# A normed input turned in 32x32 squares by VectorE and a trip through HBM instead of by TensorE

## The chip, the cores and the metric

The kernel runs on one core of one Trainium2 chip. The metric is the device time of one execution in microseconds (us), the median of several runs. Before the change it is 1411.34 us over three runs, from 1411.06 to 1411.61. All profile rows come from one profiled execution of the kernel before.

## The reference

A trunk of two layers on 512 tokens of width 1024. Cut to what matters here:

```python
def reference(x, ...):
    for i in range(2):
        xn = rmsnorm(x, norm1_g[i])             # layer 2's xn is what the change touches
        u_pool, q, k, v, g_a, g_b = split(xn @ w_in[i])
        q, k = rotary(rmsnorm(q)), rotary(rmsnorm(k))
        o = diff_attention(q, k, v, lam)        # 4 heads, chunk-causal
        merged = sigmoid(g_a) * pool_mixer(u_pool) + sigmoid(g_b) * rmsnorm(o)
        x = x + merged @ w_out[i]
        hn = rmsnorm(x, norm2_g[i])
        gate, up = split(hn @ w_ffn_in[i])
        x = x + (silu(gate) * up) @ w_ffn_out[i]
    return x
```

## The kernel before

**Tiles and products.** The 512 tokens are four tiles (0 to 3) of 128; the running sum `x` lies in SBUF as `res_88` to `res_91` (one buffer per tile). Every value that goes into a product is split into a high part and a low part (`split`: the high part is a ScalarE cast, L198; the low part a VectorE subtraction, L199), and a product of 128x1024 by 1024x512 takes 8 steps of three matmuls (`product`, L282 to L284: high by high, low weight by high, high weight by low, so that the low part of the input is first needed by the third matmul). Weights come in pieces of 128x1024 (`piece`, L212) which SP loads in the order of a plan into seven buffers; ScalarE and VectorE split them into `whi` and `wlo`.

**The handover between the layers.** The last thing layer 1 does is `ffn_out`: for each token tile it adds a finished product to `res` (L761, one add for each half of 512 columns) and then calls `normed` for that tile with the key `x1`. `normed` (L346) squares the tile with a row sum on ScalarE (L350), makes the reciprocal root by one VectorE instruction and one GpSimd power (L328, L329), scales the two halves of the tile on VectorE (L354, tile `xs`, two buffers), and defers the rest. The rest, `turn`, has TensorE transpose eight 128x128 blocks into two PSUM tiles (L303) and ScalarE and VectorE split them into `xh` and `xl`, the normed input with the width on the partitions. It is the other operand of every product in layer 2's input projection. The heads go in the order 3, 2, 1, 0 (`ORDER`), and layer 2 begins with the query and key product of head 3 for tiles 0 to 3 (`attention`, L549). Each such product ends in four squares on ScalarE (L655), a reciprocal root (L328, L329), four VectorE instructions that scale it (L659, `qn`) and a rotation.

**Who sets the order.** `later(delay, what)` puts work off until a clock that counts columns streamed by TensorE has moved on by `delay`; `need` runs it at once when something asks for its result. `normed` uses a delay of 15000 columns. The tile scheduler then sets each engine's final order by the program and its priorities, and every engine runs its own list in that order: an instruction that waits holds up all that stand behind it on its engine. SP's list holds the weight loads and all round trips through HBM.

**The other kind of transpose** is in the kernel already: `turned` (L306) has VectorE transpose 32x32 squares (L310, `near`), writes the tile to HBM (L311, `away`) and reads it back in four strips (L313), so that the squares land in their places. It is used for queries and keys, for probabilities and for head outputs, from the second head on, always with a long delay (24000 to 32000 columns) before the result is used. `squares_of` orders a destination to fit.

The attention itself scores (`scores`), turns the probabilities (`turn_prob`, splitting them into `ah` and `al`), and multiplies them by the values (`weighted`, PSUM tile `oy`), with a norm after it (L617 to L620).

Of the kernel before, what the change touches and what calls it, by code (L numbers as in the profile page):

```python
# [18 lines left out]
P = 128  # L19
# [4 lines left out]
KD = D // P  # L24
# [18 lines left out]
ORDER = (3, 2, 1, 0)  # L43
# [3 lines left out]
SCORE_WAIT, PROB_WAIT, AV_WAIT, NORM_WAIT, MERGE_WAIT = 33600, 25200, 11400, 15000, 15000  # L47
# [62 lines left out]
def trunk_kernel(  # L110
# [12 lines left out]
    nc = tc.nc  # L123
# [11 lines left out]
    def tr_ps():  # L135
        return ps.tile([P, 512], F32, name="tr", tag="tr", bufs=2)
# [59 lines left out]
    def split(hi, lo, src):  # L196

        ins = nc.scalar.copy(hi, src)  # L198
        nc.vector.tensor_sub(lo, src, hi.bitcast(F32))  # L199
        return ins  # L200
# [6 lines left out]
    def piece(raw=None):  # L207
        i = at[0]
        at[0] += 1
        if raw is None:  # L210
            raw = sb.tile([P, 2, 512], F32, name="raw", tag="raw", bufs=RAWS)
        transfers.append(nc.sync.dma_start(raw.rearrange("p a b -> p (a b)"), wts[i]))  # L212
        hi = sb.tile([P, 2, 512], F32R, name="whi", tag="whi", bufs=SPLITS)
        lo = sb.tile([P, 2, 512], F32R, name="wlo", tag="wlo", bufs=SPLITS)
        split(hi, lo, raw)
        return [(hi[:, a, :], lo[:, a, :]) for a in range(2)]
# [36 lines left out]
    def wblock(n):  # L253

        return [pair for _ in range(n // 2) for pair in piece()]
# [7 lines left out]
    def later(delay, what):  # L263
        heapq.heappush(waiting, (clock[0] + delay, count[0], what))
        count[0] += 1
# [36 lines left out]
    def transpose(dst, src):  # L302
        nc.tensor.transpose(dst, src, ident)  # L303
        clock[0] += 2 * P

    def turned(src, n, tag, bufs):  # L306

        near = sb.tile([P, n * P], F32, name="near", tag=tag, bufs=bufs)
        away = hbm.tile([P, n * P], F32, name="away", tag="away", bufs=8)
        nc.vector.transpose(near.rearrange("p (c k j) -> p k c j", c=4, k=n), src.rearrange("p (k c i) -> p k c i", k=n, c=4))  # L310
        nc.sync.dma_start(away, near)  # L311
        for c in range(4):
            nc.sync.dma_start(  # L313
                near[32 * c:32 * (c + 1), :].rearrange("i (q r) -> i q r", q=4),
                away.rearrange("(q i) (c r) -> c i q r", q=4, c=4)[c])
        return near.rearrange("p (q k j) -> p k q j", q=4, k=n)

    def squares_of(x):
        return x.rearrange("p k (q j) -> p k q j", q=4)

    def rsqrt_mean(ss, n, width, times=(1.0,), eps=None):

        r = sb.tile([P, width], F32, name="r", tag="r", bufs=4)
        part = width // len(times)
        for i, f in enumerate(times):
            cs = slice(i * part, (i + 1) * part)
            e = EPS / (f * f) if eps is None else eps[i]
            nc.vector.tensor_scalar(r[:, cs], ss[:, cs], 1.0 / (n * f * f), e, op0=ALU.mult, op1=ALU.add)  # L328
        nc.gpsimd.tensor_tensor(r, r, mhalf[:, :width], op=ALU.pow)  # L329
        return r  # L330

    def small(name, width=1):
        return sb.tile([P, width], F32, name=name, tag=name, bufs=4)

    ready = set()
# [10 lines left out]
    def normed(key, t, xh, xl, g, into=None):  # L346

        xs = sb.tile([P, D], F32, name="xs", tag="mj", bufs=2)
        ss = small("ss")
        nc.scalar.activation(xs, res[t], AF.Square, accum_out=ss)  # L350
        r = rsqrt_mean(ss, D, 1)
        for half in range(2):
            cs = slice(half * 512, (half + 1) * 512)
            nc.vector.scalar_tensor_tensor(xs[:, cs], res[t][:, cs], r, g[half], op0=ALU.mult, op1=ALU.mult)  # L354

        def turn():
            tvs = []
            for half in range(2):
                tp = oy.rearrange("p a b -> p (a b)") if t == NT - 1 and not half else tr_ps()
                for i in range(4):  # L360
                    k = half * 4 + i
                    transpose(tp[:, i * P:(i + 1) * P], xs[:, k * P:(k + 1) * P])
                tv = tp.rearrange("p (k c) -> p k c", k=4)
                tvs.append(tv)
                if into is None:
                    ks = slice(half * 4, half * 4 + 4)
                    copied = split(xh[:, ks, t * P:(t + 1) * P], xl[:, ks, t * P:(t + 1) * P], tv)
            if into is not None:
                copied = into(t, tvs)
            ready.add((key, t))  # L370
            return copied

        later(NORM_WAIT, turn)

    class Quarters:

# [46 lines left out]
    def new_xT():  # L423
        xh = sb.tile([P, KD, S], F32R, name="xh", tag="xh")
        xl = sb.tile([P, KD, S], F32R, name="xl", tag="xl")
        return xh, xl
# [30 lines left out]
    xh, xl = new_xT()  # L457
# [77 lines left out]
    for layer in range(L):  # L535
# [13 lines left out]
        def attention(j, before, then):  # L549
# [88 lines left out]
            at_start = not layer and j == ORDER[0]  # L638
            near_end = at_start or j == ORDER[-1]
            if not at_start:  # L640
                w = wblock(KD)
            for t in range(NT):
                if at_start:
                    acc = first_acc[t]
# [11 lines left out]
                r = rsqrt_mean(ss, QK, 4, (QK ** -0.5, 1.0), None if layer else [stats[:, i, t:t + 1] for i in (3, 4)])  # L656
# [14 lines left out]
            w = wblock(KD)  # L671
# [234 lines left out]
        def project_out(heads, last):  # L906
            w = [wblock(2 * len(heads)) for cb in range(2)]
            if last:
                quarters.append(Quarters())
                g = gain_row(2 * layer + 1)  # L910
                early.extend(Ffn(f0) for f0 in (0, 2))
                for f in early:
                    f.gate_raw(0)
                for f in early:
                    f.gate_raw(1)
                for f in early:
                    f.gate(0, f.n11)
                with tc.issue_after(last_merged[0].ins), tc.issue_after(last_merged[1].ins):
                    early[0].gate_in("u")
            for t in range(NT):  # L920
                for cb in range(2):
                    added = add_out([((ms[j][0][:, a, token(t)], ms[j][1][:, a, token(t)]), w[cb][2 * i + a])
                                     for i, j in enumerate(heads) for a in range(2)], t, cb)
                if last and t == 1:
                    with tc.issue_after(last_merged[0].ins), tc.issue_after(added.ins):
                        early[1].gate_in("ah", "al", "pwh", "pwl")
                if last:
                    normed(f"h{layer}", t, None, None, g, quarters[-1].put)
# [12 lines left out]
        for i, j in enumerate(ORDER):  # L941
            then = (lambda: project_out(ORDER[i - 2:i - 1], False)) if i >= 2 else None
            mjs[j] = attention(j, ORDER[i - 1] if i else None, then)
            if i:
                mix(i - 1)
# [22 lines left out]
        def ffn_out(f0, f1, last):  # L968
            nonlocal xh, xl
            for cb in range(2):  # L970
                w = wblock(f1 - f0)
                if last and cb and layer + 1 < L:
                    xh, xl = new_xT()
                    g = gain_row(2 * layer + 2)
                for t in range(NT):
                    end = last and layer == L - 1
                    add_out([((hidden[f][0][:, token(t)], hidden[f][1][:, token(t)]), w[f - f0]) for f in range(f0, f1)],
                            t, cb, 2 if end and cb and t == NT - 1 else 1, end)
                    if last and cb and not end:
                        normed(f"x{layer + 1}", t, xh, xl, g)  # L980
# [67 lines left out]
```

## Time and profile before

| | |
|---|---|
| median of three runs | 1411.34 us (1411.06 to 1411.61) |
| the profiled execution | 1411.17 us, its span 1409.4 us |
| TensorE (PE) busy | 1403.4 us |
| VectorE (DVE) busy | 1023.0 us |
| ScalarE (ACT) busy | 686.8 us |
| GpSimd (POOL) busy | 118.2 us |
| granted TensorE clock | 1.0 |

The busy times are those of the whole span. A row of the timeline reads: start in us, length in us, engine, source line, operation, output and inputs, count, and in brackets the engine's idle time just before it and what ended it. Consecutive instructions of an engine overlap in these rows (a matmul of 512 columns is listed with 0.39 us and the next one starts 0.23 us after it), so the spacing of starts is what an engine can keep up, and the length is when a result is there. "SPq" and "ACTq" are the engines as issuers of DMAs. The handover lies at about 690 to 740 us.

### The profile page before, as it was taken

To read this page: it belongs to the slowest core of one execution; us is meant where nothing else is said; L and a number is where in the kernel's file an instruction comes from. 1 tells how busy PE (TensorE), PEld (TensorE's weight loads), DVE (VectorE), ACT (ScalarE), POOL (GpSimd) and SP (SyncE) were. 2 spreads that over 40 slices of the span, in tenths; PEclk is the share of its full clock that TensorE was granted. 3 is DMA by queue.
4 is the path that set the end of the run, shared out by engine and by line. 5 is a ranking of instruction groups with operands and counts; after the bars stand their busy time and mean duration, and the time that the engine had idled before them with its cause. 6 is when DMAs were issued, how large, how long until landed. Compare 5 with 4: busy or idle time off the path is not lost.

```text
span 1409.4 us, 21870 instructions
## 1 busy us (share of the span) xinstructions
PE 1403.4 (100%) x8156; PEld 1239.0 (88%) x8156; DVE 1023.0 (73%) x1915; ACT 686.8 (49%) x1309; POOL 118.2 (8%) x144
## 2 busy tenths in 40 slices
PE   9999999999999999999999999999999999999999
PEld 7888888888999899989888888888889998999897
DVE  7779787687998548737578787767769975676462
ACT  6554343443766346526354543435447662563350
POOL 1010000100001001000010101000010000010000
PEclk9999999999999999999999999999999999999999
DMA  9345353443278357629335355434424682685351
GB/s 363 104 130 148 121 164 108 141 147 84 75 180 208 111 132 183 190 49 235 120 115 170 117 168 166 142 112 154 145 45 120 161 231 73 150 185 160 99 141 60
DMA packets 104219, 201.11 MB, mean 143 GB/s; under 512 B 32688, under 2 KB 56752, under 8 KB 104112
## 3 DMA queue, kind: packets, MB, share of 16 engines
q1 hardware_dynamic: 94176, 166.14, 36.6%
q0 software_dynamic: 8640, 31.46, 12.6%
q10 hardware_dynamic: 1296, 2.11, 0.5%
q8 instruction: 64, 1.05, 0.3%
q14 instruction: 43, 0.35, 0.1%
HBM read 183.02 MB, written 16.65 MB: 142 GB/s over the span
## 4 chain that ended last, share of the span: by engine, by line
PE 95%; DVE 2%; DMA 1%; issue 0%; POOL 0%; ACT 0%; SPq 0%; DVEq 0%; POOLq 0%; ACTq 0%
PE mm L282 19%; PE mm L284 19%; PE mm L283 19%; PE mm L296 6%; PE mm L297 6%; PE mm L294 6%; PE sc L294 3%; PE sc L297 3%; PE sc L296 3%; PE tr L297 1%; PE tr L296 1%; PE tr L294 1%; PE tr L303 1%; PE sc L284 1%; PE sc L283 1%; PE sc L282 1%
## 5 line engine op out<-in xcount | busy, mean ns | idle before, releaser
L198 ACT CAST whi<-raw 128x1024 fp32r<-128x1024 f32 (+1 forms) x225 | 234.6, 1047 | 212.6 <-issue 92.9
L199 DVE TENSOR_TENSOR wlo<-raw,whi 128x1024 fp32r<-128x1024 f32 (+1 forms) x225 | 271.8, 1215 | 74.2 <-ACT whi L198 71.5
L282 PE MATMUL mm<-whi,xh 128*128 128x512 f32 x480 | 188.7, 393 | 0.0
L283 PE MATMUL mm<-wlo,xh 128*128 128x512 f32 x480 | 187.2, 390 | 0.0
L284 PE MATMUL mm<-whi,xl 128*128 128x512 f32 x480 | 187.2, 390 | 0.0
L761 DVE TENSOR_TENSOR res<-mm,res 128x512 f32<-128x512 f32 (+1 forms) x97 | 65.7, 682 | 113.2 <-PE mm L284 113.2
L284 PE MATMUL mm<-whi,fl 128*128 128x512 f32 (+1 forms) x358 | 138.5, 387 | 0.0
L282 PE MATMUL mm<-whi,fh 128*128 128x512 f32 (+1 forms) x358 | 138.3, 387 | 0.0
L283 PE MATMUL mm<-wlo,fh 128*128 128x512 f32 (+1 forms) x358 | 138.2, 387 | 0.0
L329 POOL TENSOR_TENSOR r<-r,mhalf 128x1 f32<-128x1 f32 (+1 forms) x76 | 63.8, 840 | 614.5 <-DVE r L328 493.5
L284 PEld LDWEIGHTS mm<-whi,xl 128*128 128x128 f32 x480 | 90.1, 188 | 19.2
L283 PEld LDWEIGHTS mm<-wlo,xh 128*128 128x128 f32 x480 | 90.3, 188 | 17.4
L282 PEld LDWEIGHTS mm<-whi,xh 128*128 128x128 f32 x480 | 90.2, 188 | 17.4
L238 POOL DMA_DIRECT2D wlo<-in_wts x60 | 52.6, 876 | 604.3 <-ACT wlo L237 290.4
L282 PE MATMUL mm<-xh,whi 128*128 128x512 f32 x256 | 100.4, 392 | 0.0
L283 PE MATMUL mm<-xl,whi 128*128 128x512 f32 x256 | 99.8, 390 | 0.0
L284 PE MATMUL mm<-xh,wlo 128*128 128x512 f32 x256 | 99.8, 390 | 0.0
L296 PE MATMUL mm<-xql,whi 128*128 128x256 f32 x352 | 99.7, 283 | 0.0
L294 PE MATMUL mm<-xqh,whi 128*128 128x256 f32 x352 | 99.6, 283 | 0.0
L297 PE MATMUL mm<-xqh,wlo 128*128 128x256 f32 x352 | 99.6, 283 | 0.0
L294 PE MATMUL sc<-xqh,whi 128*128 128x256 f32 x320 | 90.7, 283 | 0.0
L294 PE MATMUL mm<-xrh,whi 128*128 128x256 f32 x320 | 90.6, 283 | 0.0
(243 smaller groups left out, 3512.1 us busy)
## 6 DMA issues: line engine op xcount, KB each, us to landing
raw<-in_wts SPq DMA_DIRECT2D x244, 512.0 KB, 4.3
wlo<-in_wts POOLq DMA_DIRECT2D x60, 512.0 KB, 7.6
away<-near SPq DMA_DIRECT2D x35, 256.0 KB, 2.4
near<-away SPq DMA_DIRECT2D x140, 64.0 KB, 2.1
away<-near SPq DMA_DIRECT2D x27, 128.0 KB, 1.8
near<-away SPq DMA_DIRECT2D x108, 32.0 KB, 2.3
xr<-in_x_t SPq DMA_DIRECT2D x4, 512.0 KB, 7.0
res<-in_x SPq DMA_DIRECT2D x4, 512.0 KB, 9.0
```

The lines of the kernel that those rows point to most:

```text
L198: ins = nc.scalar.copy(hi, src)
L199: nc.vector.tensor_sub(lo, src, hi.bitcast(F32))
L238: nc.gpsimd.dma_start(lo.rearrange("p a b -> p (a b)"), wts[piece_no], accum_op=ALU.add)
L282: nc.tensor.matmul(acc, lhsT=ah, rhs=bh, start=i == 0, stop=False)
L283: nc.tensor.matmul(acc, lhsT=ah, rhs=bl, start=False, stop=False)
L284: nc.tensor.matmul(acc, lhsT=al, rhs=bh, start=False, stop=i == n - 1)
L294: nc.tensor.matmul(acc[:, i, :], lhsT=ah, rhs=bh, start=start and not i and not k, stop=False, skip_group_check=True)
L296: nc.tensor.matmul(acc[:, i, :], lhsT=ah, rhs=bl, start=False, stop=False, skip_group_check=True)
L297: last = nc.tensor.matmul(acc[:, i, :], lhsT=al, rhs=bh, start=False, stop=i == 1 and k == 3, skip_group_check=True)
L303: nc.tensor.transpose(dst, src, ident)
L329: nc.gpsimd.tensor_tensor(r, r, mhalf[:, :width], op=ALU.pow)
L761: added = nc.vector.tensor_add(res[t][:, cs], here, res[t][:, cs])
```

## The change

`normed` for layer 2's input (the case `into is None`; the three other norms, which pass a function `into`, stay as they are) no longer uses TensorE. Right after each half of `xs` it calls `turned`: a VectorE transpose of 32x32 squares into a `near` tile, a write to HBM issued by ScalarE, and four reads issued by SP. The deferred part, `placed`, only splits from `near` into `xh` and `xl`. The `near` tiles have the tags pr0 and pr1 with two buffers each, so that tile 2 takes those of tile 0. In the second layer the loading of the query and key weights of the second head in order (head 2) is placed behind the last of these reads on SP. TensorE has 32 transposes fewer, and with them the clock that sets deferred work counts 8192 columns fewer.

```diff
-    def turned(src, n, tag, bufs):
+    returned, last_x = [], []
+
+    def turned(src, n, tag, bufs, queue=nc.sync):
...
         nc.vector.transpose(near.rearrange("p (c k j) -> p k c j", c=4, k=n), src.rearrange("p (k c i) -> p k c i", k=n, c=4))
-        nc.sync.dma_start(away, near)
+        queue.dma_start(away, near)
         for c in range(4):
-            nc.sync.dma_start(
+            returned[:] = [nc.sync.dma_start(
                 near[32 * c:32 * (c + 1), :].rearrange("i (q r) -> i q r", q=4),
-                away.rearrange("(q i) (c r) -> c i q r", q=4, c=4)[c])
+                away.rearrange("(q i) (c r) -> c i q r", q=4, c=4)[c])]
...
         r = rsqrt_mean(ss, D, 1)
+        nears = []
         for half in range(2):
             cs = slice(half * 512, (half + 1) * 512)
             nc.vector.scalar_tensor_tensor(xs[:, cs], res[t][:, cs], r, g[half], op0=ALU.mult, op1=ALU.mult)
+            if into is None:
+                nears.append(turned(xs[:, cs], 4, f"pr{half}", 2, nc.scalar))
+                last_x[:] = returned
+
+        def placed():
+            for half in range(2):
+                ks = slice(half * 4, half * 4 + 4)
+                split(*(squares_of(x[:, ks, t * P:(t + 1) * P]) for x in (xh, xl)), nears[half])
+            ready.add((key, t))
...
-                tv = tp.rearrange("p (k c) -> p k c", k=4)
-                tvs.append(tv)
-                if into is None:
-                    ks = slice(half * 4, half * 4 + 4)
-                    copied = split(xh[:, ks, t * P:(t + 1) * P], xl[:, ks, t * P:(t + 1) * P], tv)
-            if into is not None:
-                copied = into(t, tvs)
+                tvs.append(tp.rearrange("p (k c) -> p k c", k=4))
+            into(t, tvs)
             ready.add((key, t))
-            return copied
-
-        later(NORM_WAIT, turn)
+
+        later(NORM_WAIT, placed if into is None else turn)
...
             if not at_start:
-                w = wblock(KD)
+                with ExitStack() as behind:
+                    if layer and j == ORDER[1]:
+                        behind.enter_context(tc.issue_after(last_x[0].ins))
+                    w = wblock(KD)
```

How this moves instructions shows at three places. The new lines are numbered differently: L350 becomes L352, L354 becomes L357, L761 becomes L770, L328 becomes L330, L310 becomes L312, L311 becomes L313, L313 becomes L315, L655 becomes L664, L659 becomes L668.

The first place is ScalarE at the handover. Before, its list runs so (`res_88` to `res_91` are tiles 0 to 3, `tr` is the PSUM tile with the transposes):

```order
L350 ACTIVATE xs,ss<-res_88 128x1024
L350 ACTIVATE xs,ss<-res_89 128x1024
L198 CAST xh<-tr 128x4x128 x2
L350 ACTIVATE xs,ss<-res_90 128x1024
L198 CAST whi<-raw 128x1024
L198 CAST xh<-tr 128x4x128 x2
L198 CAST whi<-raw 128x1024 x2
L350 ACTIVATE xs,ss<-res_91 128x1024
```

Now it runs so (the DMA rows are the writes to HBM):

```order
L352 ACTIVATE xs,ss<-res_88 128x1024
L313 DMA away<-near 128x512 x2
L352 ACTIVATE xs,ss<-res_89 128x1024
L313 DMA away<-near 128x512 x2
L352 ACTIVATE xs,ss<-res_90 128x1024
L198 CAST xh<-near 128x4x128
L198 CAST whi<-raw 128x1024 x3
L198 CAST xh<-near 128x4x128
L313 DMA away<-near 128x512
L352 ACTIVATE xs,ss<-res_91 128x1024
L198 CAST xh<-near 128x4x128
L313 DMA away<-near 128x512
```

Each pair of writes stands in ScalarE's list between the squares of two tiles, and tile 0's first cast stands behind the squares of tile 2, where before it stood ahead of them.

The second place is VectorE at the handover. Before, from the add of tile 1 on:

```order
L761 TENSOR_TENSOR res_89<-mm,res_89 128x512
L328 TENSOR_SCALAR r<-ss 128x1
L354 SCALAR_TENSOR_TENSOR xs<-res_89,r,g 128x512 x2
L199 TENSOR_TENSOR xl<-tr,xh 128x4x128 x2
L761 TENSOR_TENSOR res_90<-mm,res_90 128x512
L706 MEMSET up 128x16 x2
L714 MEMSET us 128x16 x2
L328 TENSOR_SCALAR r<-ss 128x1
L354 SCALAR_TENSOR_TENSOR xs<-res_90,r,g 128x512 x2
L199 TENSOR_TENSOR xl<-tr,xh 128x4x128 x2
```

Now, from the transposes of tile 0 on, to tile 0's first `xl`:

```order
L312 STREAM_TRANSPOSE near<-xs 128x4x4x32 x2
L770 TENSOR_TENSOR res_89<-mm,res_89 128x512
L330 TENSOR_SCALAR r<-ss 128x1
L357 SCALAR_TENSOR_TENSOR xs<-res_89,r,g 128x512 x2
L312 STREAM_TRANSPOSE near<-xs 128x4x4x32 x2
L770 TENSOR_TENSOR res_90<-mm,res_90 128x512
L715 MEMSET up 128x16
L723 MEMSET us 128x16 x2
L715 MEMSET up 128x16
L330 TENSOR_SCALAR r<-ss 128x1
L357 SCALAR_TENSOR_TENSOR xs<-res_90,r,g 128x512
L199 TENSOR_TENSOR xl<-near,xh 128x4x128
```

And a little further on, from the scaling of tile 3 to the first `xl` of tile 2:

```order
L357 SCALAR_TENSOR_TENSOR xs<-res_91,r,g 128x512 x2
L199 TENSOR_TENSOR xl<-near,xh 128x4x128
L312 STREAM_TRANSPOSE near<-xs 128x4x4x32 x2
L330 TENSOR_SCALAR r<-ss_7446 128x2 x2
L668 SCALAR_TENSOR_TENSOR qn<-mm,r,hg 128x128 x4
L442 TENSOR_TENSOR m_7459<-qn,tab 128x128
L199 TENSOR_TENSOR xl<-near,xh 128x4x128
```

The add of the next tile stands behind the two transposes of the tile before; tile 0's low part stands behind the first scaling of tile 2; and tile 2's low part stands behind the four scalings of the first finished query and key product.

The third place is VectorE in the second layer's attention, where tile 2's probabilities of head 3 are split (`al`) and head 2's queries and keys are scaled (`qn`). Before:

```order
L328 TENSOR_SCALAR r<-sso 128x1
L310 STREAM_TRANSPOSE near<-qn 128x4x4x32
L619 SCALAR_TENSOR_TENSOR mt<-oy,r,hg 128x256
L199 TENSOR_TENSOR al<-near,ah 128x384
L620 SCALAR_TENSOR_TENSOR mt<-tb,mt 128x256
L310 STREAM_TRANSPOSE near<-mt 128x2x4x32
L328 TENSOR_SCALAR r<-ss_8042 128x2 x2
L659 SCALAR_TENSOR_TENSOR qn<-mm,r,hg 128x128 x4
```

Now:

```order
L625 SCALAR_TENSOR_TENSOR mt<-oy,r,hg 128x256
L312 STREAM_TRANSPOSE near<-qn 128x4x4x32
L626 SCALAR_TENSOR_TENSOR mt<-tb,mt 128x256
L312 STREAM_TRANSPOSE near<-mt 128x2x4x32
L330 TENSOR_SCALAR r<-ss_8067 128x2 x2
L668 SCALAR_TENSOR_TENSOR qn<-mm,r,hg 128x128 x4
L199 TENSOR_TENSOR al<-near,ah 128x384
L442 TENSOR_TENSOR m_8080<-qn,tab 128x128
```

The low part of the probabilities now stands behind the four scalings of a product that ends only when TensorE has finished it. On SP, the 32 reads of the four tiles stand together ahead of five of the six weight loads that were queued there before, and those stand ahead of the round trips of the first queries and keys.

## The prediction

> **What bounds the kernel now.** I read the page first: busy times, the granted clock, the chain that ended last. Then the table of windows, and then the timelines of TensorE, VectorE, ScalarE, GpSimd and SP around the handover. From the page, busy time by engine, the clock in 40 slices, and the chain by engine:
>
> ```profile
> PE 1403.4 (100%) x8156; PEld 1239.0 (88%) x8156; DVE 1023.0 (73%) x1915; ACT 686.8 (49%) x1309; POOL 118.2 (8%) x144
> PEclk9999999999999999999999999999999999999999
> PE 95%; DVE 2%; DMA 1%; issue 0%; POOL 0%; ACT 0%; SPq 0%; DVEq 0%; POOLq 0%; ACTq 0%
> ```
>
> TensorE is busy all the time at the full clock, and the chain is TensorE. From the windows, the handover and the first attention of layer 2 (length, then busy time of PE, PEld, DVE, ACT, POOL, clock, DMA share, GB/s):
>
> ```profile
> 690.00:740.00 50.00, 50.00 (x240) 41.60 (x238) 35.82 (x79) 23.67 (x60) 7.06 (x8) 1.00 0.35 113
> 740.00:840.00 100.00, 99.71 (x478) 83.34 (x478) 81.35 (x220) 50.06 (x137) 9.71 (x12) 1.00 0.48 149
> ```
>
> TensorE does not pause at the handover: 50.00 of 50 us. So each TensorE instruction taken away there is a gain at its full price, and each result that comes later than TensorE asks for it is a loss at its full price.
>
> **What the change removes.** The transposes in the chain (start, share of the chain in us):
>
> ```profile
> 702.18 0.87 PE tr L303 x8
> ...
> 716.52 0.44 PE oy L303 x4
> 716.95 0.44 PE tr L303 x4
> ```
>
> Tiles 0 to 2 have eight transposes for 0.87 us each, tile 3 twice four for 0.44. That is 4 x 0.88 = 3.5 us, all on the path: **-3.5 us**, if nothing else comes late.
>
> **What it adds on the way to tile 0.** Before, `xs` needs 4 us to reach TensorE's first product with it. The rows of VectorE and GpSimd, of TensorE, and of ScalarE:
>
> ```profile
> 697.25 0.15 DVE L328 TENSOR_SCALAR r<-ss 128x1 f32<-128x1 f32 x1 [1.22 <-ACT xs L350]
> 698.14 1.41 DVE L354 SCALAR_TENSOR_TENSOR xs<-res,r,g 128x512 f32<-128x512 f32 x2 [0.74 <-POOL r L329]
> 699.48 0.68 DVE L761 TENSOR_TENSOR res<-mm,res 128x512 f32<-128x512 f32 x1
> 703.58 1.28 DVE L199 TENSOR_TENSOR xl<-tr,xh 128x512 fp32r<-128x512 f32 x2
> 721.43 0.71 DVE L310 STREAM_TRANSPOSE near<-qn 128x512 f32<-128x512 f32 x1
> ```
> ```profile
> 697.55 0.56 POOL L329 TENSOR_TENSOR r<-r,mhalf 128x1 f32<-128x1 f32 x1 [36.43 <-DVE r L328]
> 717.35 1.01 POOL L329 TENSOR_TENSOR r<-r,mhalf 128x4 f32<-128x4 f32 x1 [2.38 <-DVE r L328]
> ```
> ```profile
> 702.81 0.47 PE L282 MATMUL mm<-whi,fh 128*128 128x512 f32 x1
> 703.13 0.39 PE L283 MATMUL mm<-wlo,fh 128*128 128x512 f32 x1
> 703.36 0.40 PE L284 MATMUL mm<-whi,fl 128*128 128x512 f32 x1
> 709.33 0.39 PE L282 MATMUL mm<-whi,xh 128*128 128x512 f32 x1
> ```
> ```profile
> 696.07 1.06 ACT L350 ACTIVATE xs<-res 128x1024 f32<-128x1024 f32 x1 [3.75 <-DVE res L761]
> 697.03 0.18 ACT L350 ACTIVATION_READ_ACCUMULATOR xs<-res 128x1 f32 x1
> 702.66 1.08 ACT L198 CAST xh<-tr 128x512 fp32r<-128x512 f32 x2 [1.31 <-PE tr L303]
> 708.50 2.08 ACT L198 CAST whi<-raw 128x1024 fp32r<-128x1024 f32 x2
> ```
>
> and the round trip, which this kernel makes for queries, from SP's timeline (issue of the write, issue of the reads) and from the DMA list (KB each, median us from issue to landing), with ScalarE's only kind of DMA issue so far:
>
> ```profile
> 722.17 0.33 SPq L311 DMA_DIRECT2D away<-near  x1
> 724.20 1.75 SPq L313 DMA_DIRECT2D near<-away  x4
> ```
> ```profile
> near<-away SPq DMA_DIRECT2D x140, 64.0 KB, 2.1
> ```
> ```profile
> 763.45 0.33 ACTq L696 DMA_DIRECT2D pwr<-in_pool_w  x1
> ```
>
> A write is 724.20 - 722.17 = 2.03 us until its first read goes out, four reads take 1.75 us of SP, and the last lands 2.1 us after its issue at +1.3: a round trip is 2.0 + 1.3 + 2.1 = 5.4 us. VectorE's transpose is 0.71 us long, 0.62 apart in a pair (its neighbours in the rows start 0.1 us before it ends).
>
> Tile 0: `xs` is done at 699.55, the transposes at 700.2 and 700.8, the first half's round trip at 705.7. TensorE, without the 16 transposes of tiles 0 and 1, reaches the first product with `xh` at 709.33 - 2 x 0.88 = 707.6. So the trip alone would be in time, by 1.9 us less a cast. What makes it late are the queues. ScalarE first has to issue the two writes, then to square tile 1, which waits for an add that now stands behind two transposes (700.8 instead of 699.48): add until 701.45, squares and sum 1.14 until 702.65, reciprocal root 0.15 + 0.15 + 0.56, `xs` of tile 1 from 703.6 to 705.0, its transposes until 706.2, its writes on ScalarE at 705.65 and 706.3. Only then tile 2: add until 706.8, squares until 708.0. The first cast stands behind that: 708.0 to 708.6. TensorE waits 708.65 - 707.6, some **1.1 us**. The low part stands on VectorE behind tile 2's reciprocal root and first scaling (708.2, 708.9, 709.65): 709.65 to 710.3. TensorE asks for it two matmuls of 0.23 us after the first, at 709.1: **1.2 us** more. The second half is cast behind three weight casts (0.95 us each by 2.08 for two) at 711.4 to 712.0, its low part behind a scaling, a transpose, an add and a weight split at 714.1, and TensorE asks at 713.1: **1.0 us**.
>
> **Tiles 1 to 3.** Tile 1's data has been back since 711.5 or so, and its casts come as soon as ScalarE is free: 0.1. Tile 2 shares tile 0's `near` buffers, so it could be transposed only after tile 0's `xl`; and its own `xl` stands on VectorE behind the four scalings of tile 0's query and key product, which wait for that product and what follows it:
>
> ```profile
> 715.87 0.28 ACT L655 ACTIVATE qn<-mm 128x128 f32<-128x128 f32 x1 [1.70 <-PE mm L284]
> 718.40 1.13 DVE L659 SCALAR_TENSOR_TENSOR qn<-mm,r,hg 128x128 f32<-128x128 f32 x4 [1.19 <-POOL r L329]
> ```
>
> The product ends at 707.6 + 3.3 of waits + 24 x 0.2275 = 716.4; four squares 1.1 us; the reciprocal root behind tile 3's transposes at 720.9; the power 1.2; the scalings 1.1; `xl` 0.65: 724.4. TensorE is done with tile 1 at 722.4: **2.0 us**. Tile 3's writes leave ScalarE at about 720 and its `xl` again follow scalings: 0.2 + 0.1 + 1.0 = **1.4 us** by the same steps. Handover in all: 1.1 + 1.2 + 1.0 + 0.1 + 2.0 + 1.4 = **+6.8 us**. Bounds: 0 if the casts are in time after all, 8.2 by the same steps if each landing takes 4 us (see the rivals).
>
> The five weight loads that now stand behind the 32 reads leave SP near 725 instead of before 715. They serve head 2's queries and keys, which TensorE reaches only after head 3's four query and key products and four value products, 8 x 5.5 us after 707.6, about 751: 4.3 us of landing and 2.3 of splitting are covered by 20 us.
>
> **Later in layer 2.** The clock that sets deferred work counts 8192 columns fewer, so that pieces are placed elsewhere. The one place that the trace prices is the low part `al` of head 3's tiles 2 and 3. Before:
>
> ```profile
> 771.22 0.55 DVE L199 TENSOR_TENSOR al<-near,ah 128x384 fp32r<-128x384 f32 x1
> 773.90 1.13 DVE L659 SCALAR_TENSOR_TENSOR qn<-mm,r,hg 128x128 f32<-128x128 f32 x4 [1.20 <-POOL r L329]
> ```
> ```profile
> 778.61 0.28 PE L283 MATMUL oy<-vl,ah 128*128 128x256 f32 x1
> 779.06 0.39 PE L284 MATMUL oy<-vh,al 128*128 128x256 f32 x1 [0.17 <-DVE al L199]
> ```
>
> `al` comes ahead of the scalings, and TensorE loses 0.3 us at tile 3 (0.45 us from start to start, where such matmuls follow each other in 0.12). After, tile 2's `al` stands behind the scalings of a product that ends just before TensorE wants it: squares 1.1, a backlog of about 0.7 on VectorE, power 1.2, scalings 1.1, `al` 0.6, with some 0.1 us at each of five steps from engine to engine 5.2 us after that product, while TensorE has 15 matmuls of 0.23 to do, 3.5: it waits **1.7**. Tile 3 follows likewise, behind a weight split: **0.9**, against the 0.3 of before that goes. The rest of the attention is ordered differently up to about 850 us; single waits like these there I bound by 0 and 3 us and take **1.5**, the middle, since either may be.
>
> **The sum** against the profiled execution's own 1411.17 us (span 1409.4): -3.5 + 6.8 + 1.7 + 0.9 - 0.3 + 1.5 = +7.1, so 1418.3; the median of the runs shown lies 0.2 higher, and I say **1418.4 us**.
>
> [...]
>
> **The rivals.**
>
> *Full gain (the other side).* If tile 0's chain were 2.8 us shorter, so that its first `xl` were done by 707.6, and the later `xl` came ahead of the scalings, the waits would stay at a few tenths: 1411.3 - 3.5 = 1407.8. For it speaks that the bare round trip is back at 705.7, and that ScalarE is idle for much of the stretch; it decides at tile 0's first cast, which the order puts behind tile 2's squares. Against it: that order, and the adds behind transposes.
>
> *Handover only.* The later waits vanish in slack (VectorE is idle 19 us of the 100 from 740 to 840): -3.5 + 6.8 - 0.3 = +3.0, 1414.4.
>
> *The trips are slower.* Landing is not always at its median. The lists of the write's and the reads' lines over 720 to 760 us and the whole run give, in this order:
>
> ```profile
> DMA to landing us min/median/max: 1.7/2.2/5.3
> ...
> DMA to landing us min/median/max: 1.6/2.2/6.0
> ```
>
> With 4 us for each, tile 0 is back at 709.5 and the waits add up by the same steps to 12.6, in place of 6.8 + 1.7 + 0.9 + 1.5 = 10.9: 1420.1. Eight lots of 256 KB on an otherwise half idle DMA speak against it. [...]
>
> [...]
>
> **How the numbers follow.** A measurement here tells about 0.2% (2.8 us) from no change: same is 1408.5 to 1414.2. Forecast 0.57 (own range 1416 to 1421.5), handover only 0.17, full gain 0.12, slower trips 0.09, clock 0.05. The range 1412.0 to 1422.5 takes in forecast, handover only and slower trips, and leaves out the full gain and the clock (0.17). Faster is the full gain, 0.12; same is the lower half of handover only and a little of the full gain's edge, 0.10; slower the rest, 0.78.
>
> **What would show it.** Right: no L303 row near 700; PE waits at the first `xh` and `xl`, ended by ACT and DVE, together near 7 us between 705 and 735; tile 1's squares near 701.5, tile 2's near 707; `al` waits of 1 to 2 us near 780. Wrong: PE without a pause there, or waits ended by a DMA, or a PEclk below 1.

## The result, and the profile after

The changed kernel takes 1418.86 us (median of six runs, 1418.40 to 1419.29) against 1411.32 us before: 1.0052 times, 95% interval 1.0043 to 1.0062, so 7.5 us slower. The profiled execution took 1419.0 us, its span is 1417.2.

The page's busy times, and the windows that answer to those shown of before, with the one behind them:

```profile
PE 1405.0 (99%) x8124; PEld 1236.2 (87%) x8124; DVE 1027.2 (72%) x1923; ACT 686.8 (48%) x1309; POOL 117.6 (8%) x144
```
```profile
690.00:740.00 50.00, 46.09 (x192) 36.28 (x191) 37.38 (x79) 20.75 (x49) 6.06 (x7) 0.97 0.42 137
740.00:840.00 100.00, 97.85 (x461) 80.82 (x460) 77.85 (x217) 49.68 (x142) 9.25 (x12) 1.00 0.48 150
840.00:1040.00 200.00, 199.14 (x924) 165.12 (x923) 144.24 (x341) 86.62 (x216) 13.37 (x17) 1.00 0.47 147
```

TensorE now pauses for 3.9 us at the handover, where it had none, for 2.2 in the next 100 us (0.3 before) and 0.9 in the 200 after (none before). The clock column says 0.97 for the handover: for a part of it TensorE did not run at full clock. Whom TensorE waited for, from 690 to 860 us (total, times, longest):

```profile
PE mm L284 <- DVE xl L199: 3.1, 3, 1.4
PE oy L284 <- DVE al L199: 1.9, 2, 1.3
PE mm L282 <- ACT xh L198: 0.8, 1, 0.8
PE mm L283 <- DVE wlo L199: 0.6, 1, 0.6
PE oy L284 <- DVE us L723: 0.3, 1, 0.3
PE sc L283 <- DVE ql L199: 0.2, 1, 0.2
```

What ends TensorE's waits is VectorE and ScalarE each time, never a DMA. TensorE's timeline at the handover (the number behind the start is the length of the row):

```profile
707.52 0.39 PE L284 MATMUL mm<-whi,fl 128*128 128x512 f32 x1
708.70 0.50 PE L282 MATMUL mm<-whi,xh 128*128 128x512 f32 x1 [0.79 <-ACT xh L198]
709.04 0.40 PE L283 MATMUL mm<-wlo,xh 128*128 128x512 f32 x1
710.46 0.79 PE L284 MATMUL mm<-whi,xl 128*128 128x512 f32 x1 [1.02 <-DVE xl L199]
711.05 0.63 PE L282 MATMUL mm<-whi,xh 128*128 128x512 f32 x1
711.48 0.63 PE L283 MATMUL mm<-wlo,xh 128*128 128x512 f32 x1
...
722.80 0.40 PE L283 MATMUL mm<-wlo,xh 128*128 128x512 f32 x1
724.61 0.50 PE L284 MATMUL mm<-whi,xl 128*128 128x512 f32 x1 [1.41 <-DVE xl L199]
...
734.41 0.40 PE L282 MATMUL mm<-whi,xh 128*128 128x512 f32 x1
735.50 0.50 PE L284 MATMUL mm<-whi,xl 128*128 128x512 f32 x1 [0.69 <-DVE xl L199]
```

The idle time in brackets is less than what a wait costs, because the rows' lengths overlap; from start to start the four waits take 1.18, 1.42, 1.81 and 1.09 us where 0.23 is usual, 4.6 us too much. From 710.46 on, one step from matmul to matmul takes 0.59 and the six up to 713.61 take 0.43 us each, instead of 0.23. A window over that stretch shows the granted clock at half:

```profile
710.40:713.60 3.20, 3.14 (x7) 2.48 (x8) 3.20 (x6) 2.86 (x6) 0.00 (x0) 0.50 0.59 187
```

On ScalarE (first fence; ACTq are its DMA issues, and the time before such a row in which it waits for VectorE is not shown as idle) and VectorE (second) the order of the lists can be read off:

```profile
700.46 0.93 ACTq L313 DMA_DIRECT2D away<-near  x2
701.63 1.06 ACT L352 ACTIVATE xs<-res 128x1024 f32<-128x1024 f32 x1 [4.17 <-DVE res L770]
705.76 0.92 ACTq L313 DMA_DIRECT2D away<-near  x2
706.99 1.06 ACT L352 ACTIVATE xs<-res 128x1024 f32<-128x1024 f32 x1 [4.21 <-DVE up L715]
708.05 0.60 ACT L198 CAST xh<-near 128x512 fp32r<-128x512 f32 x1
...
720.62 0.92 ACTq L313 DMA_DIRECT2D away<-near  x2
721.71 0.62 ACT L198 CAST xh<-near 128x512 fp32r<-128x512 f32 x1 [2.73 <-DMA near<-away]
```
```profile
699.72 1.30 DVE L312 STREAM_TRANSPOSE near<-xs 128x512 f32<-128x512 f32 x2
700.95 0.65 DVE L770 TENSOR_TENSOR res<-mm,res 128x512 f32<-128x512 f32 x1
...
709.05 0.75 DVE L357 SCALAR_TENSOR_TENSOR xs<-res,r,g 128x512 f32<-128x512 f32 x1 [0.72 <-POOL r L331]
709.72 0.69 DVE L199 TENSOR_TENSOR xl<-near,xh 128x512 fp32r<-128x512 f32 x1
...
722.50 1.12 DVE L668 SCALAR_TENSOR_TENSOR qn<-mm,r,hg 128x128 f32<-128x128 f32 x4 [1.19 <-POOL r L331]
...
723.86 0.69 DVE L199 TENSOR_TENSOR xl<-near,xh 128x512 fp32r<-128x512 f32 x1
```

The row at 721.71, tile 2's first cast, names a DMA as what ended ScalarE's idle time. But the four reads that this cast needs went out from 714.35 to 715.64 and landed within 2.2 us, before ScalarE was free at 719.0. What held the cast are the two writes ahead of it in the list (720.62), which waited for VectorE's transposes of tile 3.

Tile 0's trip was in time. SP's first four reads and the landing of the reads (issue to landing, minimum, median, maximum) between 699 and 727 us:

```profile
702.62 1.75 SPq L315 DMA_DIRECT2D near<-away  x4
```
```profile
DMA to landing us min/median/max: 1.8/1.9/2.7
```

The last of the four went out at 702.62 + 1.3 and landed, by the median, 1.9 later, at about 705.8: 5.4 us after the write, and 2.2 us before the cast at 708.05, which stood behind the squares of tile 2.

### The profile page after: what moved, and what is told of

It is laid out like the page before. It is cut to its first block, busy times and chain, and to the rows that moved or that the text cites. A ratio compares the mean times of both kernels' runs of the same rounds, so it can differ in the third digit from the quotient of the medians.

```text
span 1417.2 us, 21898 instructions
## 1 busy us (share of the span) xinstructions
PE 1405.0 (99%) x8124; PEld 1236.2 (87%) x8124; DVE 1027.2 (72%) x1923; ACT 686.8 (48%) x1309; POOL 117.6 (8%) x144
## 5 line engine op out<-in xcount | busy, mean ns | idle before, releaser
L770 DVE TENSOR_TENSOR res<-mm,res 128x512 f32<-128x512 f32 (+1 forms) x97 | 65.7, 681 | 113.3 <-PE mm L284 113.2
```

Source lines behind the costliest of these rows:

```text
L770: added = nc.vector.tensor_add(res[t][:, cs], here, res[t][:, cs])
```

## The experiments

Times are medians, the ratio is to the kernel before on the same chip, with its 95% interval; the changed kernel's 1418.86 us is the other mark.

**1. No turning at all.**

```diff
-                nears.append(turned(xs[:, cs], 4, f"pr{half}", 2, nc.scalar))
-                last_x[:] = returned
+                nears.append(xs[:, cs].rearrange("p (k c) -> p k c", k=4))
...
+                clock[0] += 8 * P     # in placed(), for each half
```

> Leaves out the turning of layer 2's input altogether (the high and low parts are split straight from the scaled tile, so the output is not the reference's), and lets the clock count the 8192 columns as before, so that TensorE's order is that of before without the 32 transposes. If the transposes lay on the path at 0.88 us a tile: 1411.3 - 3.5 = 1407.8 us, no wait of TensorE at the handover above 0.3 us, clock 1.00. If they were hidden or the gain is eaten by something other than lateness: 1411 us.

Measured: 1408.08 us, 0.9978 (0.9969 to 0.9987), 3.1 us faster. The handover's window:

```profile
690.00:740.00 50.00, 50.00 (x225) 41.35 (x224) 37.53 (x86) 24.38 (x61) 7.38 (x8) 1.00 0.39 127
```

This kernel also leaves out VectorE's transposes, the trip and the load order behind the reads. TensorE does not pause at the handover, and the transposes are gone from its path: the gain is real. Two waits of 0.4 and 0.5 us in the attention, against 0.2 before, cover the missing 0.4 us.

**2. Tile 0 first in the queues.**

```diff
+        with ExitStack() as behind:
+            if into is None and t == 2:
+                for ins in placed_at[0, 0]:        # tile 0's first cast and low part
+                    behind.enter_context(tc.issue_after(ins.ins))
+            nc.scalar.activation(xs, res[t], AF.Square, accum_out=ss)
+            r = rsqrt_mean(ss, D, 1)
```

> The changed kernel, with tile 2's squares queued behind tile 0's first cast on ScalarE, and tile 2's reciprocal root and first scaling behind tile 0's first low part on VectorE. Theory of the queues: tile 0's trip is back near 706, so the cast comes before 707.4 and the two waits there (0.95 and 1.19 us by start to start) and the half clock behind them (1.6 us) go, at most 1 us comes back at later tiles: 1415 to 1416 us against 1418.9. Theory that the trip itself is too long: the waits stay, ended by a DMA, 1418.9 us.

Measured: 1418.28 us, 1.0048 (1.0035 to 1.0060), near the second expectation, but by neither theory. ScalarE's list and TensorE's two waits:

```profile
706.41 1.05 ACT L198 CAST whi<-raw 128x1024 fp32r<-128x1024 f32 x1 [3.99 <-PE mm L284]
707.36 0.61 ACT L370 CAST xh<-near 128x512 fp32r<-128x512 f32 x1
707.88 1.05 ACT L356 ACTIVATE xs<-res 128x1024 f32<-128x1024 f32 x1
```
```profile
708.03 0.50 PE L282 MATMUL mm<-whi,xh 128*128 128x512 f32 x1 [0.48 <-ACT xh L370]
709.38 0.50 PE L284 MATMUL mm<-whi,xl 128*128 128x512 f32 x1 [0.61 <-DVE r L330]
```

The cast did come ahead of tile 2, at 707.36, but the scheduler put a weight cast into the gap, and that weight's low part ahead of tile 0's on VectorE. Both waits shrink, from 0.79 and 1.02 to 0.48 and 0.61 us, still without a DMA as releaser; so the trip is not the limit there. There is no half clock in the profiled execution (1.00 from 690 to 740 us). The waits for later low parts of layer 2's input are 2.4 us in four places, where the changed kernel has 2.1 in two, and the `al` waits stay (1.8 us); so little of the gain shows in the time.

**3. `al` ahead of head 2's scalings.**

```diff
+                    if layer and j == ORDER[1] and not h and last_al:
+                        behind.enter_context(tc.issue_after(last_al[0].ins))
                     nc.vector.scalar_tensor_tensor(
                         qn[:, h, :], acc[:, h * QK:(h + 1) * QK], r[:, h:h + 1], g, op0=ALU.mult, op1=ALU.mult)
```

> The changed kernel, with head 2's scalings queued behind the low parts al of head 3 on VectorE. Theory of the queues: the waits for al near 777.5 and 786.8 (1.44 and 0.85 us beyond the usual 0.12) shrink to the 0.3 of before: 1418.9 - 2.0 = 1416.9 us, the handover unchanged. Rival, that the probabilities' own round trip comes back too late there (it stands behind other DMAs on SP): the waits stay, ended by ScalarE's cast or a DMA, 1418.9 us.

Measured: 1415.89 us, 1.0032 (1.0020 to 1.0043): 3.0 us less than the changed kernel, where 2.0 was expected. From 740 to 900 us TensorE waits only

```profile
PE mm L283 <- DVE wlo L199: 0.8, 1, 0.8
PE oy L284 <- DVE us L728: 0.2, 1, 0.2
```

The waits for `al` are gone. The order in VectorE's list, not a late round trip, made them. All waits in this stretch together fall from 3.0 to 1.0 us, the 2.0 expected; the further 1.0 us between the medians was not traced.

**4. The clock counts as before.**

```diff
                 split(*(squares_of(x[:, ks, t * P:(t + 1) * P]) for x in (xh, xl)), nears[half])
+                clock[0] += 8 * P
```

> The changed kernel, with the clock that sets deferred work counting the 8192 columns of the transposes that are gone. The prediction's reason for the later waits is that the clock counts fewer columns: then the later waits (about 4.5 us from 777 to 854) go and the time is about 1414.5 us. Rival: the order on VectorE there comes from how the scheduler weighs the round trips, not from the clock; the low part al still stands behind the scalings in this kernel's list, so the time is 1417 to 1419 us.

Measured: 1419.63 us, 1.0060 (1.0047 to 1.0072). The longest entry from 740 to 900 us:

```profile
PE oy L284 <- DVE al L199: 2.3, 2, 1.8
```

The waits stay. The count of columns is not what put `al` behind the scalings. In the first experiment, which counts them too but has no trip, `al` stands ahead of them without any edit, and so it does in the fifth, which does not count them. Both leave out two things together, the trips and the load order behind the reads (the plain form of experiment 10, with one trip and no load order, also keeps the order of before). So the scheduler answers to one of these two or to both; which, and by which of its rules, was not tried.

**5. VectorE's transposes without the trip.**

```diff
+        trip = queue is nc.sync
+        if trip:
             queue.dma_start(away, near)
-        for c in range(4):
+        for c in range(4 if trip else 0):
```

> Leaves out the trip through HBM (no write, no reads; the 32x32 squares stay where VectorE turned them, so the output is not the reference's) and with it the load order behind the reads. VectorE keeps all eight transposes. Theory that the trip and what it holds up in the queues make the loss: the waits at the handover fall below 1 us in sum, 1408 to 1410 us. Rival, that VectorE's extra 5 us of transposes make it the bound at the handover: the waits for the low parts stay above 3 us in sum, 1412 to 1415 us.

Measured: 1411.40 us, 1.0001 (0.9992 to 1.0010). The handover's window:

```profile
690.00:740.00 50.00, 49.53 (x220) 40.39 (x219) 39.50 (x86) 23.61 (x60) 7.38 (x8) 1.00 0.34 110
```

VectorE has more to do there than in the changed kernel (39.5 against 37.4 us), and TensorE pauses for 0.5 us instead of 3.9. So eight transposes do not make VectorE the bound at the handover; the pause there comes with the trip, the load order and the lists that the scheduler makes for them. These three go together in this experiment and are not told apart by it. The time lies between the two expectations, because waits elsewhere appeared: 2.2 us between 740 and 840 us, ended by a probability, a head output and an `al`. So even without the trip the change gains nothing: 3.3 us of the first experiment's gain are lost with VectorE's transposes in the program (and the columns not counted), and the trip with its load order costs another 7.5.

**6. Writes on SP,** with `al` ahead as in 3.

```diff
-                nears.append(turned(xs[:, cs], 4, f"pr{half}", 2, nc.scalar))
+                nears.append(turned(xs[:, cs], 4, f"pr{half}", 2))
```

> The changed kernel with the low parts al ahead of the scalings as in the third experiment (1415.9 us), and the eight writes issued by SP instead of ScalarE. If ScalarE's queue, held by writes that wait for VectorE, makes a good part of the handover's waits (the cast of tile 2's first half, 2.7 us late): 1413 to 1414.5 us. Rival, that SP is held in the same way, with the reads behind it: 1415.5 to 1417 us.

Measured: 1424.59 us, 1.0093 (1.0079 to 1.0106), 8.7 us worse than the third experiment, worse than either expectation. SP's list:

```profile
702.21 3.64 SPq L315 DMA_DIRECT2D near<-away  x8
705.94 6.39 SPq L313 DMA_DIRECT2D away<-near  x3
712.42 3.73 SPq L315 DMA_DIRECT2D near<-away  x8
```

The third of the three writes in the middle row is tile 2's; it waits for VectorE, and tile 1's reads behind it go out at 712.42, where the changed kernel has them from 708.1. TensorE waits 9.6 us for `xh` and `xl`. After two of these waits, 0.74 us at 710.81 and 1.62 at 721.69, its clock falls to half (0.50 from 711 to 714 us, and from 722.28 to 727.40 the matmuls again follow each other in 0.43); by the spacing of the matmuls that costs some 4.4 us more, so that the 8.7 us are not the price of the held reads alone.

**7. All order edits together,** with tile 3's writes on SP.

```diff
-                nears.append(turned(xs[:, cs], 4, f"pr{half}", 2, nc.scalar))
+                nears.append(turned(xs[:, cs], 4, f"pr{half}", 2, nc.sync if t == 3 else nc.scalar))
...
+                        if layer and j == ORDER[0] and not t and not h:
+                            behind.enter_context(tc.issue_after(placed_at[2, 0][1].ins))
```

> The changed kernel with all order edits together: tile 0's first cast and low part ahead of tile 2, tile 3's writes on SP, tile 2's low part ahead of head 3's first scalings, al ahead of head 2's scalings. If queue order alone makes the loss, the handover's waits fall from about 6 to 2 us or less: 1411 to 1412.5 us. Rival, that the trip of 5.4 us plus transposes, casts and low parts leaves no slack whatever the order, so that waits come back at other tiles: 1414.5 to 1416 us.

Measured: 1423.95 us, 1.0089 (1.0076 to 1.0103). TensorE's longest wait, and ScalarE's list in front of its releaser:

```profile
730.10 0.50 PE L282 MATMUL mm<-whi,xh 128*128 128x512 f32 x1 [2.47 <-ACT xh L370]
```
```profile
728.40 0.28 ACT L672 ACTIVATE qn<-mm 128x128 f32<-128x128 f32 x1 [5.03 <-DVE near L312]
...
729.42 0.63 ACT L370 CAST xh<-near 128x512 fp32r<-128x512 f32 x1
```

Now tile 3's first cast stands behind squares that wait 5 us for VectorE to free a buffer, and TensorE's clock fell to half behind its wait (0.51 from 731 to 737 us). The time is above both expectations. The forced orders do not make this: experiment 11 has the same orders, differs only in that tile 3's writes stay on ScalarE, and takes 1414.87 us. There ScalarE's list is

```profile
723.99 0.62 ACT L370 CAST xh<-near 128x512 fp32r<-128x512 f32 x1 [0.81 <-DMA near<-away]
730.03 0.28 ACT L672 ACTIVATE qn<-mm 128x128 f32<-128x128 f32 x1 [5.42 <-DVE near L312]
```

with the cast ahead of squares that wait just as long. So the move of tile 3's two writes to SP costs 9.1 us, and what it changed in view is the place of that cast.

**8 and 10. Tile 1 alone in the new way,** in two forms: with the edit to `al` of experiment 3, and plainly.

```diff
-            if into is None:
+            if into is None and t in (1,):
                 nears.append(turned(xs[:, cs], 4, f"pr{half}", 2, nc.scalar))
...
-        later(NORM_WAIT, placed if into is None else turn)
+        later(NORM_WAIT, placed if into is None and t in (1,) else turn)
```

> The kernel before, with tile 1 alone turned in the new way (eight transposes fewer on TensorE), the clock counting its columns, and al ahead of head 2's scalings. Both theories of lateness leave tile 1 in time, since its data is back 3 us or more before TensorE wants it: 1411.2 - 0.9 = 1410.3 us, at most 0.4 us of new waits. If any trip at this place disturbs the rest: over 1411.5 us.

> Tile 1 alone in the new way as in the eighth experiment (1412.3 us), without its edit to al and without the load order behind the reads, so that VectorE and TensorE keep the order of before in the attention. If the eighth lost its 0.9 us to the edits in the attention: 1410.3 to 1410.6 us, faster than before by 0.6 to 0.9. If the trip of one tile costs it elsewhere: 1411.2 us or more.

Measured: 1412.26 us, 1.0007 (0.9999 to 1.0016), and 1412.23 us, 1.0008 (0.9999 to 1.0017). The handover is undisturbed in both; this is the plain one:

```profile
690.00:740.00 50.00, 49.90 (x235) 41.23 (x234) 37.50 (x82) 23.88 (x60) 6.55 (x8) 1.00 0.44 144
```

The tile is in time, and still the 0.9 us do not show; both second expectations hold by their times. In the plain kernel's trace TensorE waits 0.8 us for `al` after the handover, 0.2 before; that takes 0.6 of it back and leaves about 1410.9. The profiled execution took 1411.65, the lowest of eleven, so 0.8 us in it stay open, and 1.3 to the median; the interval includes no change. No version that was run and computes the whole beats the kernel before.

**9. Tile 2's low part first,** on top of experiment 3: the last two added lines of experiment 7 alone.

> The third experiment's kernel (al ahead of head 2's scalings, 1415.9 us), and tile 2's first low part ahead of the four scalings of head 3's first product on VectorE; tile 3's writes stay on ScalarE. If the place of this low part is what makes tile 2's wait of 1.6 us: the wait near 723 falls to 0.3 us or less, 1414.5 to 1415 us. Rival, that its cast, which stands behind ScalarE's waiting writes of tile 3, is the real limit: the wait stays above 1.2 us, 1415.5 to 1416 us.

Measured: 1414.54 us, 1.0023 (1.0014 to 1.0032), 1.35 us less than the third experiment. TensorE's waits in the handover are down to the two at tile 0:

```profile
708.49 0.50 PE L282 MATMUL mm<-whi,xh 128*128 128x512 f32 x1 [0.79 <-ACT xh L366]
710.24 0.50 PE L284 MATMUL mm<-whi,xl 128*128 128x512 f32 x1 [1.02 <-DVE xl L367]
```

The place behind the scalings was tile 2's wait.

**11. Tile 0 first, too,** experiments 2 and 9 together.

> The ninth experiment's kernel, with tile 0's first cast and low part ahead of tile 2's squares and scaling as in the second experiment. If order edits add up: the waits at tile 0 and tile 2 are both small, 1413 to 1414 us. If each moves its wait to a later tile, as in the second and seventh experiments: 1414.5 to 1416.5 us, with waits for low parts in tiles 1 to 3.

Measured: 1414.87 us, 1.0028 (1.0017 to 1.0039), no better than the ninth. VectorE's low parts are late six times:

```profile
PE mm L284 <- DVE xl L371: 3.4, 6, 1.0
```

The edits do not add up, as the second expectation has it. Bringing tile 0 forward delays tile 2's scaling (710.06, in the changed kernel 709.05), and with it, it seems, what follows.

## Why the prediction was right, point by point

- **The gain, -3.5 us.** Shown by experiment 1: 3.1 us, with waits of 0.9 us in the attention against 0.2 before.
- **Tile 0, 1.1 + 1.2 + 1.0 us.** From start to start the first two waits cost 0.95 and 1.19 us, ended by the cast behind tile 2's squares and the low part behind tile 2's scaling, as forecast; the times of the rows agree within 0.2 us (cast 708.0 forecast, 708.05 in the trace; trip 5.4 us in both). The third did not appear in this execution: the half clock slowed TensorE by 1.6 us over the stretch in which it would have waited. Experiment 4, with the same lists at the handover and full clock (1.00 from 690 to 740 us), shows that wait with 0.58 us in its row, 0.74 from start to start.
- **Tiles 1 to 3, 0.1 + 2.0 + 1.4 us.** Measured: none, 1.6 (1.7 with the slow step behind it), 0.9. Experiment 9 shows that the scalings held up tile 2's low part. Two sums of the working do not come out: the terms for tile 2 behind 720.9 (1.2, 1.1 and 0.65) lead to 723.85 and not 724.4, so to some 1.4 us in place of 2.0, and tile 3's 0.2 + 0.1 + 1.0 is 1.3. That ScalarE's waiting writes also held tile 2's cast (721.71) was not in the working; experiment 9's cast comes hardly earlier (721.50), and the wait is gone, so it did not decide.
- **Head 3's `al`, 1.7 + 0.9 us.** Measured 1.44 and 0.85 beyond the usual 0.12, at 779.1 and 787.8. The mechanism is shown by experiment 3.
- **The rest of the attention, 1.5 us.** Measured 2.6 from start to start (a late `wlo` near 852 with 0.74 and slow steps behind it, the rest in waits of 0.2 to 0.5), less 0.4 that the kernel before loses in the same stretch: 2.2. The forecast took the middle of a bound of 0 to 3 us and named no place, so that it came near is luck.
- **The reason given for the later waits** was wrong: "The clock that sets deferred work counts 8192 columns fewer, so that pieces are placed elsewhere." With the count restored, experiment 4 keeps them. The two `al` places came out because they were read from the lists themselves.
- **The rivals.** *Full gain* decided at tile 0's first cast, and that came late. *Handover only* failed by the 4 us after the handover. *Slower trips*: landing was 1.9 us at the median at the handover and 2.2 over the run, and no wait of TensorE was ended by a DMA. The clock had 0.05 among the chances, which was the author's estimate: the trace of before has 1.00 at the handover and shows no fall. A fall happened in small: the forecast's own sign of being wrong, a clock below 1, is there at the handover (0.97), behind waits with 0.79 and 1.02 us in their rows. Its price was 1.6 us over 3.2 us of half clock. In exchange 1.0 of forecast waits went, so that the time hardly moved.

The sum against the measurement, from start to start: at the handover 5.0 us of waits with the slow step behind each, and 1.6 of half clock; later 4.2 more than before; less 3.5. That makes 7.3, and the time moved by 7.5.

The mechanism, in-order lists in which a result stands behind something that waits, is shown by experiment 3 for `al` (1.9 us of waits in the changed kernel, none there) and by experiment 9 for tile 2 (a row with 1.41 us of waiting in the changed kernel, none there). At tile 0 it is read from the lists, and experiment 2, which changed them only in part, took away 0.7 of the 1.8 us. That the total came within 0.5 us is in part luck: tile 2, tile 3 and a third wait at tile 0 were put 1.9 us too high together, and a half clock of 1.6 us that was not in the sum and 0.7 us more in the rest of the attention made up for it. The waits at the handover, forecast at 6.8 us and named as a sign at near 7, were 5.0.

## What to carry to other kernels

In this kernel, whose bounding engine had no pause at the handover (busy 50.00 of 50 us before), a cheaper instruction elsewhere was paid by where its producers and consumers stand in the in-order lists: tile 0's data was back 2.2 us ahead of its cast and was used late, because casts and low parts stood behind squares and scalings that waited for something else. Read the new lists with the old trace's durations before measuring; that gave the places and times of the first waits within 0.2 us. Order edits at this saturated place moved waits as well as removed them (experiment 11 waits 3.4 us for low parts, six times, where the ninth waits 1.0 us once), so price an edit by the whole stretch and not by the wait that it removes.

## What the runs showed of the hardware

The granted clock of TensorE fell to half after short pauses: two pauses of 0.8 and 1.0 us (rows at 708.70 and 710.46) were followed by 3.2 us at a clock of 0.50. In the profiled executions of experiments 3 and 4 the same two pauses at the same place were followed by no fall, and in that of experiment 9 by one again. The window from 711 to 714 us, first in experiment 3, then in experiment 9:

```profile
711.00:714.00 3.00, 2.43 (x11) 1.69 (x10) 3.00 (x5) 2.44 (x5) 0.00 (x0) 1.00 0.51 167
711.00:714.00 3.00, 3.00 (x8) 2.31 (x8) 3.00 (x5) 2.46 (x5) 0.00 (x0) 0.50 0.52 170
```

So whether such a pause cost clock differed from execution to execution. The changed kernel's own six executions agree with that: their mean granted clock reads 0.999 in three (1418.78 to 1419.29 us) and 1.000 in three (1418.40 to 1418.93 us). What decides it, no run shows.
